# Experts in order of token count, and both parts of the activations in one stationary operand for three of them

## The chip, the cores and the metric

The kernel runs on one core of a Trainium2 chip. The metric is the device time of one execution in microseconds. TensorE (PE, with its weight loads PEld), VectorE (DVE), ScalarE (ACT), GpSimd (POOL) and SyncE (SP, which only issues transfers here) run at the same time and wait for each other by semaphores.

## What is computed

Two layers of an encoder on 256 tokens of 1,024 columns. Each layer has a mixer; layer 0 has a dense network behind it, layer 1 a mixture of eight experts, and the change is in that alone:

```python
def moe_swiglu(h, router_w, w1, w3, w2):
    t = h.reshape(B * L, D)
    logits = (t @ router_w).astype(jnp.float32)
    top_val, top_idx = lax.top_k(logits, TOP_K)
    top_w = jax.nn.softmax(top_val, axis=-1)
    ...
    for e in range(N_EXPERTS):
        out = out + combine[:, e:e + 1] * swiglu(t, w1[e], w3[e], w2[e])
```

`TOP_K` is 2 and `N_EXPERTS` 8. `swiglu` is `(silu(h @ w1) * (h @ w3)) @ w2`, with 3,584 hidden columns per expert. All is float32.

## The kernel before

**Split operands.** A float32 operand is split into a high part in a reduced type and the rest, the low part. A product is then three matmuls: high by high, high by low, low by high. Weights come in tiles of 128 x 1,024 (512 KB, `raw`), loaded on SyncE's queue (`wload`, line 286). ScalarE casts the high part (`wh`, line 319) and VectorE subtracts it for the low part (`wl`, line 320). There are four buffers for each part in the expert stage, so a tile's cast waits until TensorE is done with the tile four before. `take` (line 377) splits ahead until four tiles are ready.

**Loads.** The order of the loads is the plan written by `plan_experts`. For the raw tiles there are 16 permanent buffers and, by `lend` (line 1730), others for a time; four of these serve until tile 640 of the 672, so loads run 20 tiles ahead in most of the stage.

**Gather.** An expert has 128 slots. `one_hot` (line 1668) makes, from each token's slot, a matrix of 0 and 1 on VectorE. `gather` (line 1775) multiplies the tokens with it, two experts at a time, which gives each expert's tokens as stationary operands `gx`, high and low. It runs as a side task, a step every few products, during the last three blocks of the expert ahead. Behind the first gather, `weights` (line 1743) makes the softmax weights and `total` (line 1735) the counts; if one expert has more than 128 tokens, `over` is set and a second pass is run under an `If`, which comes last in the program.

**Blocks.** For each expert `e` and each `b` of 7 blocks of 512 hidden columns there are 4 tiles of w1 and 4 of w3 (lines 1891 to 1893, 48 matmuls of 512 columns). `gated` makes the activations `ma`: a SiLU on ScalarE, a product on VectorE (line 1902). `turned` (line 1847) transposes those of the block before with four matmuls, casts the high part on ScalarE and subtracts on VectorE (line 1854). `down` (line 1814) multiplies them with 4 tiles of w2 into `my` (lines 1820 to 1822, 24 matmuls). At an expert's end `weighted` splits and scales the result (VectorE line 1830) and `scatter` adds it to the tokens with 8 matmuls and 4 adds on VectorE (line 1845), spread over the next expert's second block.

**Order.** TensorE, VectorE and ScalarE run in the order in which the code is written (`by_hand`); SyncE's order is the scheduler's.

## Time and profile before

| | |
|---|---|
| median of 3 runs | 1926.29 us (1923.55 to 1928.28) |
| the profiled execution | 1928.92 us, of which its span 1927.1 us |
| PE / PEld busy | 1877.5 us (97%) / 1575.1 us (82%) |
| DVE / ACT / POOL busy | 1609.8 us (84%) / 1329.1 us (69%) / 29.7 us (2%) |
| matmuls of lines 1891 to 1893 | 3 x 896, starting at 925.4 us |
| matmuls of lines 1820 to 1822 | 3 x 448 |
| low parts on DVE, line 320 | 893, 1222 ns in the mean |
| high parts on ACT, line 319 | 893, 1053 ns in the mean |
| HBM read | 528.02 MB, mean of the span 275 GB/s |

The span runs from the first to the last instruction. A matmul's own time overlaps with that of the next: its duration (some 0.39 us for 512 columns) is no price, the step from one start to the next is. The share of DMA engines' time can go over 1, since packets overlap.

### The profile page before, as it was taken

The page shows a single profiled execution, that of the slowest core. Times are in us where ns is not written, and L with a number is a line of the kernel's source. Part 1 is how long each engine was busy: PE and PEld are TensorE (multiplying, and loading weights), DVE is VectorE, ACT ScalarE, POOL GpSimd, SP SyncE. Part 2 cuts the span into 40 slices and gives each one's busy share as a digit, 9 for nine tenths or more (in the row PEclk, how much of TensorE's full clock was granted, in tenths as well). Part 3 has the DMA queues.
Part 4 walks back from the last instruction along what each step waited for, and adds up shares of the span by engine and source line. Part 5 has one row for each costly group of instructions (what it writes and reads, how often), then busy time and mean ns, then how long its engine had stood idle before and what let it go on. Part 6 is the DMA issues. An engine that isn't in the chain of part 4 may idle for free.

```text
span 1927.1 us, 32350 instructions
## 1 busy us (share of the span) xinstructions
PE 1877.5 (97%) x12152; PEld 1575.1 (82%) x12152; DVE 1609.8 (84%) x2013; ACT 1329.1 (69%) x1874; POOL 29.7 (2%) x54
## 2 busy tenths in 40 slices
PE   7999999999989999999999999999999999999997
PEld 6987788799879877787788888888888888888885
DVE  6887887777766888767899989999889998899997
ACT  4785466643356874675777787777877778877775
POOL 1000000000000000000000000000000000000000
PEclk9999999999999999999999999999999999999998
DMA  9545765478874457568899999999999999999993
GB/s 326 162 132 159 237 184 183 149 252 271 278 231 132 142 159 227 184 200 321 277 335 351 339 350 344 365 375 356 354 339 368 368 354 369 338 352 378 357 324 108
DMA packets 258018, 531.29 MB, mean 276 GB/s; under 512 B 22126, under 2 KB 45116, under 8 KB 257852
## 3 DMA queue, kind: packets, MB, share of 16 engines
q1 hardware_dynamic: 257500, 528.99, 79.6%
q8 instruction: 97, 1.59, 0.3%
q14 instruction: 69, 0.57, 0.1%
q0 software_dynamic: 192, 0.07, 0.0%
q10 hardware_dynamic: 160, 0.07, 0.0%
HBM read 528.02 MB, written 1.05 MB: 275 GB/s over the span
## 4 chain that ended last, share of the span: by engine, by line
PE 75%; DMA 9%; DVE 7%; ACT 6%; issue 2%; SPq 0%; POOL 0%; ACTq 0%; DVEq 0%; POOLq 0%
PE mo L1891 11%; PE mo L1893 11%; PE mo L1892 11%; PE my L1820 5%; PE my L1821 5%; PE my L1822 5%; PE pn L398 3%; PE pn L401 3%; DMA raw<-in_ffn_w 3%; PE pn L399 3%; DVE wl L320 3%; DMA raw<-in_adaln_w 3%; PE pt L437 2%; PE pt L438 2%; PE pt L439 2%
## 5 line engine op out<-in xcount | busy, mean ns | idle before, releaser
L320 DVE TENSOR_TENSOR wl<-raw,wh 128x1024 fp32r<-128x1024 f32 (+1 forms) x893 | 1076.8, 1222 | 164.6 <-ACT wh L319 127.6
L319 ACT CAST wh<-raw 128x1024 fp32r<-128x1024 f32 (+1 forms) x893 | 931.8, 1053 | 375.5 <-PE mo L1893 97.9
L1891 PE MATMUL mo<-wh,gx 128*128 128x512 f32 x896 | 357.0, 398 | 0.0
L1892 PE MATMUL mo<-wl,gx 128*128 128x512 f32 x896 | 351.0, 392 | 0.0
L1893 PE MATMUL mo<-wh,gx 128*128 128x512 f32 x896 | 350.9, 392 | 0.0
L1893 PEld LDWEIGHTS mo<-wh,gx 128*128 128x128 f32 x896 | 168.2, 188 | 38.6 <-ACT gx L1792 1.2
L1891 PEld LDWEIGHTS mo<-wh,gx 128*128 128x128 f32 x896 | 168.4, 188 | 34.7 <-ACT gx L1792 0.6
L1892 PEld LDWEIGHTS mo<-wl,gx 128*128 128x128 f32 x896 | 168.5, 188 | 34.5 <-DVE wl L320 0.2
L1820 PE MATMUL my<-wh,aTm 128*128 128x512 f32 x448 | 176.0, 393 | 0.0
L1821 PE MATMUL my<-wl,aTm 128*128 128x512 f32 x448 | 175.3, 391 | 0.0
L1822 PE MATMUL my<-wh,aTm 128*128 128x512 f32 x448 | 175.2, 391 | 0.0
L438 PE MATMUL pt<-xH,wl 128*128 128x256 f32 x576 | 164.1, 285 | 3.7 <-DVE wl L320 3.6
L437 PE MATMUL pt<-xH,wh 128*128 128x256 f32 x576 | 166.4, 289 | 0.0
L439 PE MATMUL pt<-xL,wh 128*128 128x256 f32 x576 | 163.6, 284 | 0.0
L398 PE MATMUL pn<-wh,xH 128*128 128x512 f32 x352 | 149.1, 424 | 0.0
L399 PE MATMUL pn<-wl,xH 128*128 128x512 f32 x352 | 138.6, 394 | 0.0
L401 PE MATMUL pn<-wh,xL 128*128 128x512 f32 x352 | 138.6, 394 | 0.0
L450 DVE SCALAR_TENSOR_TENSOR acc<-raw,scol,acc 128x512 f32<-128x512 f32 x140 | 104.7, 748 | 26.7 <-DMA raw<-in_adaln_w 25.1
L438 PEld LDWEIGHTS pt<-xH,wl 128*128 128x128 f32 x576 | 111.1, 193 | 4.9 <-DVE wl L320 4.7
L437 PEld LDWEIGHTS pt<-xH,wh 128*128 128x128 f32 x576 | 111.1, 193 | 0.3
L439 PEld LDWEIGHTS pt<-xL,wh 128*128 128x128 f32 x576 | 111.1, 193 | 0.0
L1822 PEld LDWEIGHTS my<-wh,aTm 128*128 128x128 f32 x448 | 84.1, 188 | 18.9
(451 smaller groups left out, 2515.2 us busy)
## 6 DMA issues: line engine op xcount, KB each, us to landing
raw<-in_moe_w SPq DMA_DIRECT2D x672, 512.0 KB, 5.3
raw<-in_w_in SPq DMA_DIRECT2D x128, 512.0 KB, 3.8
raw<-in_adaln_w SPq DMA_DIRECT2D x80, 512.0 KB, 4.5
raw<-in_ffn_w SPq DMA_DIRECT2D x66, 512.0 KB, 4.7
raw<-in_w_branch SPq DMA_DIRECT2D x24, 512.0 KB, 3.9
rawe<-in_adaln_w SPq DMA_DIRECT2D x16, 512.0 KB, 7.3
raw<-in_w_out SPq DMA_DIRECT2D x16, 512.0 KB, 4.3
x<-in_x SPq DMA_DIRECT2D x2, 512.0 KB, 6.4
```

What stands on the lines that cost most here:

```text
L319: S.copy(H, r)
L320: low = lambda: tt(L, r, H, op=OP.subtract)
L398: mm(o, xH[:, tb, k, :], H, start=k == 0, stop=False)
L437: mm(d, H[:, cs], xH[:, :, k, :], start=k == 0 and c % 2 == 0, stop=False, skip_group_check=True)
L438: mm(d, L[:, cs], xH[:, :, k, :], start=False, stop=False, skip_group_check=True)
L439: mm(d, H[:, cs], xL[:, :, k, :], start=False, stop=k == KD - 1, skip_group_check=True)
L1820: mm(y[hf], aT[:, 0, k, :], H[:, c], start=b == 0 and k == 0, stop=False)
L1821: mm(y[hf], aT[:, 0, k, :], L[:, c], start=False, stop=False)
L1822: mm(y[hf], aT[:, 1, k, :], H[:, c], start=False, stop=b == nb - 1 and k == 3)
L1891: mm(q, gH[:, k, :], H, start=k == 0, stop=False)
L1892: mm(q, gH[:, k, :], L, start=False, stop=False)
L1893: mm(q, gL[:, k, :], H, start=False, stop=k == KD - 1)
```

## The change

The experts are taken in another order. Expert 0 stays first; the others follow by falling token count. The new `order`, in the place of `total`, ranks the counts on VectorE, makes a permutation, writes the expert numbers into `idx` and puts slots, masks and weights into the new order. `expert_rows` loads weights by an address from a register, which SyncE reads from `idx`; the seven reads and the one of `over` stand in SyncE's order ahead of the 38th tile's load (w3, expert 0, block 3), whose buffer is that of the 11th tile.

The last three places (5 to 7) use 64 slots. Their one-hot matrix holds the 64 slots twice, so `gx`, and all products up to the activations, have each token in row s and again in row s + 64. `turned` then takes the high part from the first 64 columns and the low part from the second, into one stationary operand of 128 columns, and `down` has two matmuls, by the weights' high and low part, in place of three. The scatter adds both halves of the rows. `over` is now set if the largest count is over 128 or that of place 5 is over 64. The first gather is for expert 0 alone, since the order isn't known then, and the second for place 1 alone; three pairs follow.

```diff
-    def plan_experts():
+    def expert_rows(w, e, sorted_, c0, n, k0, kn):
+        if not (sorted_ and e):
+            return kview(A[w][0, e], c0, n, k0, kn)
+        if e not in which:
+            which[e] = nc.values_load(idx[0:1, e:e + 1], engines=(E.SP,), min_val=0, max_val=NE - 1)
+        return A[w][0, bass.ds(which[e], 1), k0 * P:(k0 + kn) * P, c0:c0 + n].rearrange("o (k p) n -> p (o k) n", p=P)
+    def plan_experts(sorted_):
...
                 for w in ("moe_w1", "moe_w3"):
-                    add(w, lambda k0, kn, w=w, e=e, b=b: kview(A[w][0, e], b * 512, 512, k0, kn), KD, 512)
+                    add(w, lambda k0, kn, w=w, e=e, b=b: expert_rows(w, e, sorted_, b * 512, 512, k0, kn), KD, 512)
...
-        def one_hot(slots, pr):
+        def one_hot(slots, m, es, half):
...
+                for j, e in enumerate(es):
+                    at, o = C("iota"), hot[tb][:, j, :]
+                    if e in half:
+                        at = at[:, None, 0:64].to_broadcast([P, 2, 64])
+                        o = o.rearrange("p (i s) -> p i s", i=2)
+                    ts(o, at, slots[:, tb, e:e + 1], m[:, tb, e:e + 1], op0=OP.is_equal, op1=OP.mult)
             return hot
...
-            hots = [one_hot(slot, 0)]
+            hots = [one_hot(slot, m01, (0,), ())]
...
-        def total():
+        slotP, m01P, combP = [cvT[:, i:i + 2 * NE].rearrange("p (t e) -> p t e", t=2) for i in (0, 16, 32)]
+        first_slot = cvT[:, 48:48 + NE]
+        BIG = 5
+        def order():
...
             o = ps("total", [P, NE])
             mm(o, ones, m01[:, 0, :], start=True, stop=False)
             mm(o, ones, m01[:, 1, :], start=False, stop=True)
-            V.tensor_reduce(most, o, axis=AX.X, op=OP.max)
-            ts(over, most, float(P) + 0.5, None, op0=OP.is_gt)
+            n, pos, at = [tl("cnt", [P, NE], "ms") for _ in range(3)]
+            V.tensor_copy(n, o)
+            V.tensor_reduce(most[:, 0:1], n, axis=AX.X, op=OP.max)
+            ts(n[:, 0:1], n[:, 0:1], 1024.0, None, op0=OP.add)
+            sq = lambda t: (t[:, None, :].to_broadcast([P, NE, NE]), t[:, :, None].to_broadcast([P, NE, NE]))
+            nf, ne = sq(n)
+            gt, ge = [tl("gt", [P, NE, NE], "gq") for _ in range(2)]
+            tt(gt, nf, ne, op=OP.is_gt)
+            tt(ge, nf, ne, op=OP.is_ge)
+            V.copy_predicated(gt, C("tri8").bitcast(U32).rearrange("p (e f) -> p e f", e=NE), ge)
+            V.tensor_reduce(pos, gt, axis=AX.X, op=OP.add)
+            ts(first_slot, pos, BIG - 0.5, -64.0, op0=OP.is_gt, op1=OP.mult)
+            ts(first_slot, first_slot, 128.0, None, op0=OP.add)
+            perm, u = [tl("perm", [P, NE, NE], "gq") for _ in range(2)]
+            tt(perm, sq(pos)[0], sq(C("iota")[:, 0:NE])[1], op=OP.is_equal)
+            tt(u, perm, sq(C("iota")[:, 0:NE])[0], op=OP.mult)
+            V.tensor_reduce(at, u, axis=AX.X, op=OP.add)
+            V.tensor_copy(idx, at)
+            u = tl("permn", [P, NE], "ms")
+            tt(u, perm[:, BIG, :], n, op=OP.mult)
+            V.tensor_reduce(most[:, 1:2], u, axis=AX.X, op=OP.add)
+            ts(most[:, 1:2], most[:, 1:2], 64.0, most[:, 0:1], op0=OP.add, op1=OP.max)
+            ts(over, most[:, 1:2], float(P) + 0.5, None, op0=OP.is_gt)
+            u = tl("permu", [P, 2, NE, NE], "l1")
+            for d, s in ((slotP, slot), (m01P, m01), (combP, combk)):
+                tt(u, perm[:, None, :, :].to_broadcast([P, 2, NE, NE]),
+                   s[:, :, None, :].to_broadcast([P, 2, NE, NE]), op=OP.mult)
+                V.tensor_reduce(d, u, axis=AX.X, op=OP.add)
...
-            slots = slot
+            slots, m, comb, half = slotP, m01P, combP, range(BIG, NE)
             if blk:
-                plan_experts()
-                slots = tl("slb", [P, 2, NE], "gs")
-                ts(slots, slot, float(-P * blk), None, op0=OP.add)
+                plan_experts(False)
+                slots, m, comb, half = tl("slb", [P, 2, NE], "gs"), m01, combk, ()
+                tt(slots, slot, first_slot[:, None, :].to_broadcast([P, 2, NE]), op=OP.subtract)
             nb = DE // 512
-            def gather(pr, every):
-
-                hot = hots.pop(0) if hots else one_hot(slots, pr)
-                if pr:
+            groups = deque(((0,), (1,), (2, 3), (4, 5), (6, 7)))
+            def gather(es, every):
+                if es[0]:
                     yield 16
-                gs = [[tl("gx", [P, KD, P], "e4", F32R) for _ in range(2)] for _ in range(2)]
-                hT = [tl("hT", [P, 2, P], "l1", F32R) for _ in range(2)]
+                n = len(es)
+                gs = [[tl("gx", [P, KD, P], "e4", F32R) for _ in range(2)] for _ in es]
+                hT = [tl("hT", [P, 2, P], "l1", F32R) for _ in es]
...
                 for k in range(0, KD, 2):
                     for part, src in enumerate((hH, hL)):
-                        o = ps("gx", [P, 2, 2, P])
+                        o = ps("gx", [P, 2, n, P])
                         for i in range(2):
                             for tb in range(2):
                                 mm(o[:, i], src[:, tb, (k + i) * P:(k + i) * P + P], hot[tb],
                                    start=tb == 0, stop=tb == 1)
-                        S.copy(gs[0][part][:, k:k + 2, :], o[:, :, 0, :])
-                        S.copy(gs[1][part][:, k:k + 2, :], o[:, :, 1, :])
+                        for j in range(n):
+                            S.copy(gs[j][part][:, k:k + 2, :], o[:, :, j, :])
                         if part == 0:
...
-                if pr == 0 and slots is slot:
+                if es[0] == blk == 0:
                     weights()
-                    total()
+                    order()
                     yield 8
                 ws = ps("ws", [P, 2])
-                o = ps("hTp", [P, 2, 2, P])
-                for j in range(2):
-                    e = 2 * pr + j
+                o = ps("hTp", [P, n, 2, P])
-                        mm(ws[:, j:j + 1], hot[tb][:, j, :].bitcast(F32), combk[:, tb, e:e + 1],
+                        mm(ws[:, j:j + 1], hot[tb][:, j, :].bitcast(F32), comb[:, tb, e:e + 1],
...
                     for hf in range(2):
                         c = slice(hf * 512, hf * 512 + 512)
-                        mm(y[hf], aT[:, 0, k, :], H[:, c], start=b == 0 and k == 0, stop=False)
-                        mm(y[hf], aT[:, 0, k, :], L[:, c], start=False, stop=False)
-                        mm(y[hf], aT[:, 1, k, :], H[:, c], start=False, stop=b == nb - 1 and k == 3)
+                        first, last = b == 0 and k == 0, b == nb - 1 and k == 3
+                        if e in half:
+                            mm(y[hf], aT[:, k, :], H[:, c], start=first, stop=False)
+                            mm(y[hf], aT[:, k, :], L[:, c], start=False, stop=last)
+                        else:
+                            mm(y[hf], aT[:, 0, k, :], H[:, c], start=first, stop=False)
+                            mm(y[hf], aT[:, 0, k, :], L[:, c], start=False, stop=False)
+                            mm(y[hf], aT[:, 1, k, :], H[:, c], start=False, stop=last)
...
-            def turned(t):
+            def turned(e, t):
                 q = ps("maT", [P, 4, P])
                 for k in range(4):
                     nc.tensor.transpose(q[:, k, :], t[:, k * P:k * P + P], ident)
+                if e in half:
+                    aT = tl("aTm", [P, 4, P], "m4", F32R)
+                    S.copy(aT[:, :, 0:64], q[:, :, 0:64])
+                    tt(aT[:, :, 64:128], q[:, :, 64:128], aT[:, :, 0:64], op=OP.subtract)
+                    return aT
                 aT = tl("aTm", [P, 2, 4, P], "m4", F32R)
                 S.copy(aT[:, 0], q)
...
-            first = gather(0, 1)
+            first = gather(groups.popleft(), 1)
             for e in range(NE):
                 for b in range(nb):
-                    if e % 2 and b == 4 and e + 1 < NE:
-                        more = Side(gather(e // 2 + 1, 4), 1)
-                    if e and e % 2 == 0 and b == 0:
+                    if b == 4 and groups and groups[0][0] == e + 1:
+                        more = Side(gather(groups.popleft(), 4), 1)
+                    if e and b == 0:
                         more.drain("gather")
...
-    plan_experts()
+    plan_experts(True)
```

On VectorE, around the counts of the first gather (`oh`, `rest` and `combk` belong to the softmax weights, `wl` is the low part of the next weight tile), there stood:

```order
L1764 TENSOR_TENSOR combk<-oh_10315,rest_10320 128x16
L1740 TENSOR_REDUCE most<-total_10335 128x1
L1741 TENSOR_SCALAR over<-most 128x1
L320 TENSOR_TENSOR wl_10341<-raw_9946,wh_10340 128x1024
L1902 TENSOR_TENSOR ma_10350<-ma_10350,mo_10284 128x512
```

and now stands:

```order
L1811 TENSOR_TENSOR combk<-oh_10303,rest_10308 128x16
L1760 COPY cnt_10326<-total_10323 128x8
L1761 TENSOR_REDUCE most<-cnt_10326 128x1
L1762 TENSOR_SCALAR cnt_10326<-cnt_10326 128x1
L1766 TENSOR_TENSOR gt_10332<-cnt_10326 128x64
L1767 TENSOR_TENSOR gt_10333<-cnt_10326 128x64
L1768 COPY_PREDICATED gt_10332<-cc,gt_10333 128x64
L1769 TENSOR_REDUCE cnt_10327<-gt_10332 128x8
L1771 TENSOR_SCALAR cvT<-cnt_10327 128x8
L1772 TENSOR_SCALAR cvT<-cvT 128x8
L1775 TENSOR_TENSOR perm_10340<-cnt_10327,cc 128x64
L1776 TENSOR_TENSOR perm_10341<-perm_10340,cc 128x64
```

with 12 more such operations behind, of which six have 128 elements a partition or reduce these, and only then the low part of the same weight tile.

On TensorE, in a block of one of the last experts, between the last tile of w3 (`mo`) and the second tile of w2, there stood:

```order
L1893 MATMUL mo_17738<-wh_17741,gx_16618 128x512
L1820 MATMUL my_17315<-wh_17753,aTm_17735 128x512
L1821 MATMUL my_17315<-wl_17754,aTm_17735 128x512
L1822 MATMUL my_17315<-wh_17753,aTm_17735 128x512
L1820 MATMUL my_17316<-wh_17753,aTm_17735 128x512
L1821 MATMUL my_17316<-wl_17754,aTm_17735 128x512
L1822 MATMUL my_17316<-wh_17753,aTm_17735 128x512
L1820 MATMUL my_17315<-wh_17764,aTm_17735 128x512
```

and now stands:

```order
L1953 MATMUL mo_18707<-wh_18710,gx_16721 128x512
L1872 MATMUL my_18457<-wh_18722,aTm_18704 128x512
L1873 MATMUL my_18457<-wl_18723,aTm_18704 128x512
L1872 MATMUL my_18458<-wh_18722,aTm_18704 128x512
L1873 MATMUL my_18458<-wl_18723,aTm_18704 128x512
L1872 MATMUL my_18457<-wh_18734,aTm_18704 128x512
```

that is, two matmuls per tile and half of the output in place of three.

## Rows read from the trace of the kernel before

**Rows 1.** Stretch, length, busy (count): PE, PEld, DVE, ACT, POOL; clock, DMA share, GB/s.
```profile
1500.00:1550.00 50.00, 50.00 (x226) 41.01 (x225) 46.24 (x42) 39.65 (x42) 0.00 (x0) 1.00 1.01 374
```

**Rows 2.** Timeline of PE over one block: start, length, line, operation, tiles, shape, count.
```profile
1499.73 0.39 PE L1820 MATMUL my<-wh,aTm 128*128 128x512 f32 x1
...
1503.83 0.40 PE L1891 MATMUL mo<-wh,gx 128*128 128x512 f32 x1
...
1509.34 0.60 PE L1851 MATMUL maT<-cc,ma 128*128 128x128 f32 x4
...
1520.81 0.40 PE L1891 MATMUL mo<-wh,gx 128*128 128x512 f32 x1
```

**Rows 3.** Waits from 880 us on: total us, times, longest us.
```profile
ACT wh L319 <- PE mo L1893: 97.9, 290, 0.8
...
ACT wh L319 <- DMA raw<-in_moe_w: 1.3, 4, 0.3
```

**Rows 4.** Timeline of DVE in plain blocks: start, length, last the idle time before.
```profile
1504.90 0.68 DVE L1902 TENSOR_TENSOR ma<-ma,mo 128x512 f32<-128x512 f32 x1
1505.50 4.99 DVE L320 TENSOR_TENSOR wl<-raw,wh 128x1024 fp32r<-128x1024 f32 x4
1510.60 0.69 DVE L1854 TENSOR_TENSOR aTm<-maT,aTm 128x512 fp32r<-128x512 f32 x1
...
1557.71 3.49 DVE L320 TENSOR_TENSOR wl<-raw,wh 128x1024 fp32r<-128x1024 f32 x3
```

**Rows 5.** Groups by line on DVE: count, busy us, mean ns, idle before.
```profile
L1845 DVE TENSOR_TENSOR acc<-acc,sc 128x512 f32<-128x512 f32 x32 | 21.8, 681 | 0.1
...
L1830 DVE SCALAR_TENSOR_TENSOR ywL<-my,wsl,ywH 128x512 fp32r<-128x512 f32 x16 | 11.3, 744 | 3.2 <-ACT ywH L1829 3.2
```

**Rows 6.** Timeline of DVE in the router, ahead of the experts.
```profile
920.22 0.17 DVE L1645 COPY lgs<-lg 128x8 f32<-128x8 f32 x1 [0.56 <-PE lg L1641]
...
921.33 0.17 DVE L1653 TENSOR_SCALAR m<-rank 128x8 f32<-128x8 f32 x1
...
922.67 1.11 DVE L1673 TENSOR_SCALAR hot<-cc,slot,m 128x128 fp32r<-128x128 f32 x4
```

**Rows 7.** Timeline of DVE at the total of the counts.
```profile
942.51 0.16 DVE L1740 TENSOR_REDUCE most<-total 128x1 f32<-128x8 f32 x1
...
942.78 1.23 DVE L320 TENSOR_TENSOR wl<-raw,wh 128x1024 fp32r<-128x1024 f32 x1
```

**Rows 8.** Waits from 936 to 972 us.
```profile
PEld mo L1892 <- DVE wl L320: 0.2, 1, 0.2
```

**Rows 9.** Timeline of PE: full-precision matmuls of 128 columns, reduced ones of 256.
```profile
252.62 1.61 PE L1313 MATMUL do<-dv,aT 128*128 128x128 f32 x13
...
927.16 0.64 PE L1790 MATMUL gx<-hot,hH 128*128 128x256 f32 x4
```

**Rows 10.** Stretches around a fall of the clock, columns as in rows 1.
```profile
363.00:367.40 4.40, 1.85 (x14) 1.42 (x13) 2.95 (x8) 3.99 (x11) 0.55 (x1) 1.00 0.02 4
367.40:371.00 3.60, 3.60 (x19) 3.60 (x20) 2.44 (x5) 2.02 (x5) 0.92 (x1) 0.56 0.00 0
```

**Rows 11.** Stretches with a full DMA queue, and the fastest plain one.
```profile
880.00:890.00 10.00, 9.86 (x52) 8.06 (x51) 8.16 (x12) 3.32 (x6) 0.00 (x0) 1.00 1.05 402
...
1260.00:1280.00 20.00, 20.00 (x94) 16.42 (x93) 18.51 (x17) 15.50 (x16) 0.00 (x0) 1.00 1.02 379
```

**Rows 12.** DMA issues: tile, queue, count, KB each, us to landing.
```profile
raw<-in_moe_w SPq DMA_DIRECT2D x672, 512.0 KB, 5.3
```

**Rows 13.** Instructions of SyncE: shortest, median, longest ns.
```profile
L286 SPq DMA_DIRECT2D raw<-in_moe_w x672: 327/368/1355, 871.6 to 1886.1; - x168
...
L1940 SPq TENSOR_LOAD <-over x1: 480/480/480, 1886.4 to 1886.4; - x1
```

**Rows 14.** Timeline of DVE and of PE at the end.
```profile
1905.37 3.60 DVE L320 TENSOR_TENSOR wl<-raw,wh 128x1024 fp32r<-128x1024 f32 x3
...
1911.73 0.39 PE L1822 MATMUL my<-wh,aTm 128*128 128x512 f32 x1
```

More of the change, by code (lines that the diff above doesn't have):

```diff
@@ L1606, in moe_pool_a @@
             slots_of[tag].append((a, b))
-    def plan_experts():
+    which = {}
+    idx = cst.tile([P, NE], I32, name="idx")
+    def expert_rows(w, e, sorted_, c0, n, k0, kn):
[5 more added lines that the diff above has]
+    def plan_experts(sorted_):
         nb = DE // 512
@@ L1666, in nat_lo @@
             tt(hL[:, tb, c], hns[tb, q].rearrange("p a b -> p (a b)"), hH[:, tb, c], op=OP.subtract)
-        def one_hot(slots, pr):
-            hot = [tl("hot", [P, 2, P], "l1", F32R) for _ in range(2)]
+        def one_hot(slots, m, es, half):
+            hot = [tl("hot", [P, len(es), P], "l1", F32R) for _ in range(2)]
             for tb in range(2):
-                for j in range(2):
-                    e = 2 * pr + j
-                    ts(hot[tb][:, j, :], C("iota"), slots[:, tb, e:e + 1], m01[:, tb, e:e + 1],
-                       op0=OP.is_equal, op1=OP.mult)
+                for j, e in enumerate(es):
[4 more added lines that the diff above has]
+                    ts(o, at, slots[:, tb, e:e + 1], m[:, tb, e:e + 1], op0=OP.is_equal, op1=OP.mult)
             return hot
@@ L1730, in moe @@
             lend([10000] * 16 + [70] * 2 + [640] + [131] * 2 + [640] * 3 + [84] + [60] * 2)
-        most = cst.tile([P, 1], F32, name="most")
+        most = cst.tile([P, 2], F32, name="most")
         over = cst.tile([P, 1], I32, name="over")
-        def total():
+        slotP, m01P, combP = [cvT[:, i:i + 2 * NE].rearrange("p (t e) -> p t e", t=2) for i in (0, 16, 32)]
+        first_slot = cvT[:, 48:48 + NE]
+        BIG = 5
+        def order():
             o = ps("total", [P, NE])
@@ L1766, in experts @@
         def experts(blk):
[L1768 removed]
+            slots, m, comb, half = slotP, m01P, combP, range(BIG, NE)
             if blk:
[L1770 to L1772 removed]
+                plan_experts(False)
+                slots, m, comb, half = tl("slb", [P, 2, NE], "gs"), m01, combk, ()
+                tt(slots, slot, first_slot[:, None, :].to_broadcast([P, 2, NE]), op=OP.subtract)
             nb = DE // 512
[L1775 to L1778 removed]
+            groups = deque(((0,), (1,), (2, 3), (4, 5), (6, 7)))
+            def gather(es, every):
+                hot = hots.pop(0) if hots else one_hot(slots, m, es, half)
+                if es[0]:
                     yield 16
[L1780 to L1781 removed]
+                n = len(es)
+                gs = [[tl("gx", [P, KD, P], "e4", F32R) for _ in range(2)] for _ in es]
+                hT = [tl("hT", [P, 2, P], "l1", F32R) for _ in es]
                 wsl = tl("wsl", [P, 2], "ms")
[L1783 to L1784 removed]
+                for j, e in enumerate(es):
+                    of[e] = gs[j], hT[j], wsl[:, j:j + 1]
                 for k in range(0, KD, 2):
                     for part, src in enumerate((hH, hL)):
[L1787 removed]
+                        o = ps("gx", [P, 2, n, P])
                         for i in range(2):
@@ L1796, in gather @@
                     yield every
-                if pr == 0 and slots is slot:
+                if es[0] == blk == 0:
                     weights()
-                    total()
+                    order()
                     yield 8
                 ws = ps("ws", [P, 2])
-                o = ps("hTp", [P, 2, 2, P])
-                for j in range(2):
-                    e = 2 * pr + j
+                o = ps("hTp", [P, n, 2, P])
+                for j, e in enumerate(es):
                     for tb in range(2):
-                        mm(ws[:, j:j + 1], hot[tb][:, j, :].bitcast(F32), combk[:, tb, e:e + 1],
+                        mm(ws[:, j:j + 1], hot[tb][:, j, :].bitcast(F32), comb[:, tb, e:e + 1],
                            start=tb == 0, stop=tb == 1)
@@ L1809, in gather, with down @@
                         nc.tensor.transpose(o[:, j, tb, :], hot[tb][:, j, :].bitcast(F32), ident)
-                for j in range(2):
+                for j in range(n):
                     S.copy(hT[j], o[:, j])
-                S.copy(wsl, ws)
-            def down(y, b, aT, then=None):
+                S.copy(wsl[:, 0:n], ws[:, 0:n])
+            def down(e, b, aT, then=None):
+                y = ys[e]
                 for k, H, L in pieces("moe_w2", 4):
@@ L1860, in end @@
                     ys[e] = [ps("my", [P, 512], "pg") for _ in range(2)]
[L1861 removed]
+                down(e, b, aT, then)
                 if b == nb - 1:
@@ L1910, in experts @@
                     if prev is not None:
-                        end(prev[0], prev[1], aT, 2, (lambda: aTs.append(turned(t))) if final else None)
+                        end(prev[0], prev[1], aT, 2, (lambda: aTs.append(turned(e, t))) if final else None)
                     if not final:
```

7 lines of the change are left out of this document (2 added, 5 removed).

## The prediction

> **What bounds the kernel now.** I read the busy time by stretch first. In the 50 us from 1500, a plain part of the expert stage, TensorE is busy all the time, VectorE 46.24 us, ScalarE 39.65 us, the clock is granted in full, and the DMA engines move 374 GB/s at a share of 1.01 [rows 1]. Three resources are near their end at once, so the order of the waits decides. The waits say that ScalarE waits for TensorE to give a weight buffer back (97.9 us, 290 times), and hardly ever for a transfer (1.3 us, 4 times) [rows 3]: TensorE sets the pace and the others follow it. The timeline of TensorE gives its prices [rows 2]. One block (one expert, 512 of its hidden columns) lasts from 1503.83 to 1520.81, 16.98 us, and holds 72 matmuls of 512 columns, 4 transposes and no gap. Eighteen matmuls of the product with w2 take 1503.83 - 1499.73 = 4.10 us, 0.228 us each. So a matmul that goes is worth 0.228 us as long as nobody else is late.
>
> **What goes.** Three experts have 7 blocks each, and each block loses 8 of its 24 matmuls with w2: 3 x 7 x 8 = 168 matmuls, 168 x 0.228 = **-38.3 us**. A block of these experts becomes 16.98 - 8 x 0.228 = 15.16 us on TensorE.
>
> **What is late next in such a block.** Each of the others must do the same 12 tiles of weights in 15.16 us.
> ScalarE's share of a block is 39.65 / 50 x 16.98 = 13.5 us; it fits.
> VectorE: 12 low parts, one product of the gate, one low part of the activations. Back to back the low parts take 3.49 / 3 = 1.16 us each; where ScalarE's casts come in between, 4.99 / 4 = 1.25 us [rows 4]. The gate's product is 0.68. The low part of the activations is 0.69 at 512 columns and now has 256, so between 0.35 and 0.69; I take 0.43, nearer to the half. Back to back the sum is 12 x 1.16 + 0.68 + 0.43 = 15.0 us, just under 15.16; at 1.25 it is 16.1. I take 1.16, since a late engine is one that finds its input ready.
> VectorE has more in two blocks of every expert: the adds of the scatter, 4 x 0.68 = 2.7 us, in the second one, and the two weighted outputs, 2 x 0.74 = 1.5 us, in the first one [rows 5]. With the scatter, VectorE needs 15.0 + 2.7 = 17.7 us against 15.16 + 8 x 0.228 = 17.0 on TensorE; with the weighted outputs 16.5 against 15.2. The scatters of three experts and the weighted outputs of two fall into shortened blocks: 3 x 0.7 + 2 x 1.3 = 4.7 us at most, nothing if the four buffers of split weights bridge it. I take **+3.0**.
> The transfers: 12 tiles of 512 KB are 6.29 MB, in 15.16 us 415 GB/s. Where its queue was full the kernel moved 402 GB/s [rows 11], which makes 15.65 us a block, 0.49 too slow, 21 x 0.49 = 10.3 us over the three experts. But the loads run 20 buffers ahead (16 for good and four until tile 640), which is 20 x 16.98 / 12 = 28.3 us, of which 5.3 go from issue to landing [rows 12]. The lead of 23 us is larger than 10.3, so I cost the transfers at **0**.
> The end: VectorE's last three low parts start at 1905.37 and end at 1908.97 and the last matmul of the last product starts at 1911.73 [rows 14]. The 16 matmuls that go from the last two products would put it at 1908.1, before its weights are split. VectorE ends some 0.3 us earlier than now and leaves three matmuls, so it starts at about 1908.7 + 0.2 + 2 x 0.228 = 1909.3 and 1.2 us of the 168 matmuls' worth are lost: **+1.2** (0 to 2).
>
> **What is added: the order.** The new function puts 23 small operations on VectorE where 2 stood, ahead of the next low part. Six such operations of the ranking, of 8 to 64 elements, go from 920.22 to 921.50, 0.21 us each; four of 128 elements take 1.11 us, 0.28 each [rows 6]. Seventeen are of the first kind and six of the second: 17 x 0.21 + 6 x 0.28 = 5.3 us. The two that go took 942.78 - 942.51 = 0.27 [rows 7]. Net 5.0 us (4 to 6.5). Nothing hides it: behind the same place TensorE already waits 0.2 us for that low part today [rows 8], so its store of split weights is used up there. **+5.0.** In that wait TensorE stands still for 5 us. From 363 to 367.4 it was busy for 1.85 of 4.40 us, and over the next 3.6 us the granted clock was 0.56 in the mean, that is some 3.2 us at 1.2 GHz in place of 2.4 [rows 10]. Half the clock for 3.2 us costs 1.6 us. **+1.6** (0 if the clock holds, 3.2 if it stays low twice as long).
>
> **What is added: one more gather.** The first two experts are gathered alone, each with 32 matmuls of 128 columns in place of 32 of 256 for both. Four of 256 columns take 0.64 us, of which the last has 0.28, so one each 0.12; no such matmul of 128 columns with the reduced type is in the trace. Below, it could cost half of 0.12; above, as much as one of 512, 0.23. The nearest row is the full-precision one, where every record has 128 columns: 13 in 1.61, (1.61 - 0.28) / 12 = 0.11 [rows 9]. I take that: 64 x 0.11 - 32 x 0.12 = **+3.2** (0 to 64 x 0.23 - 3.8 = 10.9). The Trainium skill prices a stream of load-and-multiply pairs of 128 columns at 81 ns (TensorE: Matmul & The Clock Gate, Back-to-back issue gap); by that estimate the term would be 64 x 0.081 - 3.8 = +1.3. No row here shows that price; the nearest is the 0.11 above, of another type.
> In the first block each step has half of ScalarE's copies now. That can only gain, by tenths of a microsecond a step; I cost it at 0.
>
> **What moves at no cost.** SyncE reads seven expert numbers and the overflow flag right behind the order instead of the flag at the end. A read takes 0.48 us, and with the register work behind it perhaps 0.8: 8 x 0.8 = 6.4 us, in which the loads behind stand. The first of them would have waited for the low part behind the order anyway, and has a lead of over 20 tiles; cover gone, 6 us at most. Seven of eight experts' 588 loads take a register for their address; an issue takes 0.37 us now, in 1.26 us per tile there is room for three times that [rows 13]. The narrower cast of the activations on ScalarE lies beside the matmuls with w3, as now.
>
> **Sum.** -38.3 + 3.0 + 1.2 + 5.0 + 1.6 + 3.2 = -24.3 us. The profiled execution took 1928.92 us, its span being 1927.1, and would take 1904.6. The median of the three runs is 1926.29, 2.6 lower than the profiled one, and a change in the expert stage carries over as it is: **1902 us**.
>
> **Rivals.**
> A. *The short matmuls are dear.* If a matmul of 128 columns costs as much as one of 512, the extra gather is 10.9 in place of 3.2: 1902 + 7.7 = 1909. Against it stands only the row of another type.
> B. *VectorE becomes the bound.* At 1.25 us per low part a shortened block is 16.1, not 15.16: 21 x 0.95 = 20 us, 1922; with half of it, 1912. For it: 46.24 of 50 us busy [rows 1]. Against: many of the present steps of 1.25 hold a wait for ScalarE.
> C. *The DMA engines become the bound.* At 379 GB/s, the best 20 us of the plain part [rows 11], a block is 16.6 us; 21 x 1.44 = 30 us, less the lead of 23: 1902 + 7 = 1909. Had the stage no lead, only 21 x 0.38 = 8.0 us would come from the shortened blocks, and 1926.3 - 8.0 + 9.8 = 1928. The 402 GB/s with a full queue speak against it. The Trainium skill puts a core's share of HBM at about 358 GB/s and the vendor's figure at 368 (DMA: Bandwidth & Descriptors, Specifications); by 368 a block would need an estimated 17.1 us, as long as now, nothing would be gained and the time would be 1926.3 + 9.8 = 1936. The trace disagrees, with 374 over 50 us and 402 over 10.
> D. *SyncE becomes the bound, and the kernel slower.* If issuing a load with an address from a register takes longer than the 1.41 us in which tiles are used today, the seven experts go at its pace: at 1.6 us per load 588 x 0.19 = 112 us more, about 2040. It eats the gain from 1.26 us on and turns the sign at some 1.45. For it: the longest issue of these loads is 1.36 us; against it: their median is 0.37 [rows 13].
> E. *The change doesn't do what it says.* If the sixth expert in the order had over 64 tokens, everything would run twice. The reference's inputs give the experts 31, 45, 104, 80, 61, 72, 33 and 86 tokens; the first stays first, so the sixth has 61. Nothing runs twice.
>
> **How the numbers follow.** The forecast, with TensorE as the bound and the short matmuls at 0.11, 0.51; A 0.24; B 0.10; C with the lead 0.08; C without it 0.03; D 0.03; E 0.01. Predicted is the forecast's 1902; with its own terms at their ends (no stall of the clock, no loss on VectorE; or all of them) it lies between 1893 and 1908. The range takes in A, C with the lead and half of B: 1892 to 1915; what is left out is the rest of B, D, E and C without a lead, about 0.15. A measurement of this kernel tells 0.3% (5.8 us) from no change. Faster: forecast, A, B and C with the lead, 0.93. Within 0.3%: C without the lead, 0.03. Slower: D and E, 0.04.
>
> **What would show it.** The period of a plain block of the last three experts should be 15.2 us, with ScalarE still waiting for TensorE; 15.7 to 16.6 with the low parts back to back and TensorE waiting for them is B, the same with ScalarE waiting for transfers is C. The first five experts' plain blocks should stay at 16.98. At the order TensorE should stand for some 5 us and the clock fall once. The 128-column gather should step by 0.11 us, in A by over 0.2. SyncE should still wait for free buffers, not issue without a pause. The forecast is wrong above all if the shortened blocks do not come near 15.2.

## The result, and the profile after

The changed kernel takes 1901.0 us in the median (1900.1 to 1902.2), the kernel before 1926.97 in the same comparison: a ratio of 0.9863, with an interval from 0.9844 to 0.9882. The forecast was 1902. The profiled execution has a span of 1899.4 us (1927.1 before). Most of the forecast's steps held. Under the good agreement lie two errors in opposite directions: some 3 us in the terms of the sum, and 4 to 8 us from something that the forecast didn't have. That the number came out within 1 us is luck. The experiments take the two apart.

I divide the expert stage into blocks by the start of the first matmul with w1 (lines 1951 and, before, 1891), and read it from the timeline of TensorE. All in us; "stage" is from the first such matmul to the end of the span. Ahead of it, the profiled runs below differ by up to 11.5 us (918.7 to 930.2) where their instructions are the same, so the stage tells more than the median. Part of it goes with the clock: up to 918 us the granted clock is 0.98 in the mean in e2's profiled execution, the longest ahead of the stage, and 1.00 in e6's, the shortest.

| kernel | median | stage | first expert | its 2nd block | plain block | shortened | shortened, scatter |
|---|---|---|---|---|---|---|---|
| before | 1926.97 | 1001.6 | 118.7 | 18.23 | 16.96 | | |
| after | 1901.0 | 972.3 | 129.0 | 25.09 | 16.81 | 15.0 | 18.03 |
| e1 32 bytes at the left | 1922.27 | 993.9 | 117.8 | 18.17 | 16.81 | | |
| e2 no 32 bytes | 1905.45 | 980.3 | 130.9 | 25.27 | 16.96 | 15.15 | 18.05 |
| e3 three products | 1935.3 | 1005.0 | 129.0 | 24.98 | 16.81 | | |
| e4 spread order | 1892.13 | 965.2 | 121.6 | 16.83 | 16.81 | 15.0 | 18.04 |
| e5 seven short | 1857.64 | 928.1 | 129.3 | 25.34 | 16.80 | 15.0 | 18.03 |
| e6 spread, 32 bytes at the right | 1890.95 | 965.4 | 121.6 | 16.83 | 16.81 | 15.0 | 18.04 |
| e7 fill the stall | 1896.55 | 969.8 | 126.4 | 17.83 | 16.81 | 15.0 | 18.03 |
| e8 32 bytes at the right | 1919.9 | 994.2 | 117.9 | 18.18 | 16.81 | | |
| e9, e10, e11 | 1929.53, 1927.8, 1926.74 | 1004.3, 1002.2, 1000.1 | 119.1, 118.9, 118.5 | 18.2 to 18.3 | 17.02, 16.98, 16.92 | | |

The busy time by stretch, as [rows 1], of the changed kernel at the order, in a plain part with three products and in the shortened part:

```profile
943.50:949.00 5.50, 1.77 (x8) 1.13 (x6) 4.88 (x25) 4.56 (x5) 0.00 (x0) 1.00 0.44 168
949.00:956.00 7.00, 6.09 (x19) 5.00 (x20) 5.83 (x6) 1.38 (x3) 0.00 (x0) 0.51 0.54 175
1500.00:1550.00 50.00, 50.00 (x228) 41.38 (x227) 46.49 (x43) 39.84 (x42) 0.00 (x0) 1.00 1.02 375
1700.00:1750.00 50.00, 50.00 (x227) 41.24 (x226) 49.22 (x48) 42.95 (x47) 0.00 (x0) 1.00 1.03 390
```

In the shortened part TensorE is still busy all the time and at the full clock; VectorE has risen from 46.49 to 49.22 of 50 us, the transfers from 375 to 390 GB/s. One shortened block on TensorE, as [rows 2]:

```profile
1708.87 0.40 PE L1951 MATMUL mo<-wh,gx 128*128 128x512 f32 x1
...
1723.88 0.39 PE L1951 MATMUL mo<-wh,gx 128*128 128x512 f32 x1
```

15.01 us. VectorE in it, as [rows 4]:

```profile
1711.08 0.68 DVE L1962 TENSOR_TENSOR ma<-ma,mo 128x512 f32<-128x512 f32 x1
1711.68 4.62 DVE L320 TENSOR_TENSOR wl<-raw,wh 128x1024 fp32r<-128x1024 f32 x4
1716.22 0.42 DVE L1910 TENSOR_TENSOR aTm<-maT,aTm 128x256 fp32r<-128x256 f32 x1
1716.55 9.62 DVE L320 TENSOR_TENSOR wl<-raw,wh 128x1024 fp32r<-128x1024 f32 x8
```

The low parts follow each other without a gap, 4.62 / 4 = 1.16 and 9.62 / 8 = 1.20 us each, and the shorter low part of the activations takes 0.42 (the forecast had 1.16 and 0.43). The block from one gate product to the next (1711.08 to 1726.09) is 15.0 us on VectorE too.

The waits from 880 us on, as [rows 3]:

```profile
ACT wh L319 <- PE mo L1953: 80.4, 242, 0.8
...
PEld mo L1952 <- DVE wl L320: 11.2, 15, 5.1
...
ACT wh L319 <- DMA raw<-in_moe_w: 2.3, 6, 0.8
```

ScalarE still waits for TensorE, and for a transfer six times. Of TensorE's waits for a low part, 5.1 us are one wait. It stands behind the order; TensorE and then VectorE there, as [rows 6 to 8]:

```profile
944.89 0.39 PE L1951 MATMUL mo<-wh,gx 128*128 128x512 f32 x1
949.91 0.80 PE L1952 MATMUL mo<-wl,gx 128*128 128x512 f32 x1 [4.64 <-DVE wl L320]
950.50 0.63 PE L1953 MATMUL mo<-wh,gx 128*128 128x512 f32 x1
```

```profile
943.50 0.16 DVE L1760 COPY cnt<-total 128x8 f32<-128x8 f32 x1
943.69 0.16 DVE L1761 TENSOR_REDUCE most<-cnt 128x1 f32<-128x8 f32 x1
...
948.44 0.29 DVE L1788 TENSOR_REDUCE cvT<-permu 128x16 f32<-128x128 f32 x1
948.64 1.22 DVE L320 TENSOR_TENSOR wl<-raw,wh 128x1024 fp32r<-128x1024 f32 x1
```

The 23 operations last from 943.50 to 948.64, 5.14 us (5.3 forecast). TensorE stands idle for 4.64 us, and then its matmuls step by 0.43 in place of 0.23: the granted clock of the 7 us behind is 0.51, its 1.2 GHz level.

SyncE's reads of the order, and its issues of the experts' loads, as [rows 13]:

```profile
L1616 SPq TENSOR_LOAD <-idx x7: 262/267/474, 946.2 to 949.9; - x7
```

```profile
L286 SPq DMA_DIRECT2D raw<-in_moe_w x672: 327/373/1297, 872.9 to 1862.5; - x168
L286 SPq FUSED_REGOPS  x588: 42/46/61, 1017.2 to 1861.5; - x196
L286 SPq MOVE raw<-in_moe_w x588: 29/29/37, 1017.3 to 1861.6; - x196
```

The issue itself keeps its price with an address from a register (0.373 us, 0.368 before), and two small instructions of 0.046 and 0.029 stand ahead of it: together 0.45 us of the 1.25 that a tile has in a shortened block.

### The profile page after: what moved, and what is told of

It reads as the page before. It is cut to its first block, busy times and chain, and to the rows that moved or that the text cites. A ratio compares the mean times of both kernels' runs of the same rounds, so it can differ in the third digit from the quotient of the medians.

```text
span 1899.4 us, 33296 instructions
## 1 busy us (share of the span) xinstructions
PE 1841.5 (97%) x12016; PEld 1547.4 (81%) x12016; DVE 1597.5 (84%) x2034; ACT 1321.2 (70%) x1875; POOL 28.1 (1%) x54
## 4 chain that ended last, share of the span: by engine, by line
PE 75%; DMA 9%; DVE 7%; ACT 6%; issue 2%; POOL 0%; SPq 0%; DVEq 0%; ACTq 0%; POOLq 0%
PE mo L1952 11%; PE mo L1951 11%; PE mo L1953 11%; PE pn L398 4%; PE pn L401 4%; PE pn L399 4%; PE my L1875 3%; PE my L1876 3%; PE my L1877 3%; DMA raw<-in_adaln_w 3%; DMA raw<-in_ffn_w 3%; DVE wl L320 3%; ACT wh L319 2%; PE my L1873 2%; PE my L1872 2%
## 5 line engine op out<-in xcount | busy, mean ns | idle before, releaser
L1951 PEld LDWEIGHTS mo<-wh,gx 128*128 128x128 f32 x896 | 168.9, 188 | 32.8 <-ACT gx L1842 0.5
L1875 PE MATMUL my<-wh,aTm 128*128 128x512 f32 x280 | 109.1, 390 | 0.0
L1876 PE MATMUL my<-wl,aTm 128*128 128x512 f32 x280 | 109.0, 389 | 0.0
L1877 PE MATMUL my<-wh,aTm 128*128 128x512 f32 x280 | 108.9, 389 | 0.0
L398 PEld LDWEIGHTS pn<-wh,xH 128*128 128x128 f32 x352 | 66.9, 190 | 19.3 <-issue 7.6
```

The lines of the kernel that those rows point to most:

```text
L398: mm(o, xH[:, tb, k, :], H, start=k == 0, stop=False)
L1875: mm(y[hf], aT[:, 0, k, :], H[:, c], start=first, stop=False)
L1951: mm(q, gH[:, k, :], H, start=k == 0, stop=False)
```

## The experiments

Four questions: why plain blocks fell to 16.81 us where the forecast had them unchanged (e1, e2, e8 to e11), what the short products are worth by themselves (e3), what the order costs and whether it must (e4, e6, e7), and whether VectorE or the transfers come next (e5).

**e1: 32 bytes in the kernel before.** The row of indices is a new tile in the pool of constants, and the pools on its side move up by 32 bytes; the fourth of the four pairs of split buffers lies in a pool that fills the memory from the other end and stays.

```diff
+    pad = cst.tile([P, NE], I32, name="idx")
     def plan_experts():
```

> The kernel before with nothing added but 32 unused bytes per partition in the pool of constants, where the change puts its row of indices. That moves three of the four buffers for high and for low parts, and all that lies above them, by 32 bytes against the fourth. Theory PLACE (the plain block fell from 16.96 to 16.81 us since the buffers moved): the plain block here takes 16.81, the eight experts lose about 1.06 us each, and the kernel takes about 1918.5 us. Theory STREAM (it fell through the changed instructions or the addresses read from registers): the block stays at 16.96 and the time at 1926 to 1927.

The plain block took 16.81 us, the stage 993.9 in place of 1001.6; the median, 1922.27, was 0.9978 of before (0.9967 to 0.999), 4 us short of what was expected, with the stage as expected. PLACE holds: the change's 32 bytes alone bring 7.7 us in the stage.

**e2: the change without the 32 bytes.**

```diff
-    idx = cst.tile([P, NE], I32, name="idx")
+    idx = cvT[:, 56:56 + NE].bitcast(I32)
```

> The changed kernel with the row of indices kept in a spare part of a tile that is there already, so that no buffer moves against the kernel before. Theory PLACE: plain blocks with three products go back from 16.81 to 16.96 us, those with two from 15.0 to about 15.15, and the time rises from 1901 to about 1909. Theory STREAM: 16.81, 15.0 and 1901.

16.96 and 15.15 us, a stage of 980.3, and 1905.45 us: 0.9875 of before (0.9844 to 0.9907). So the change as it is described is worth 21.2 us in the median and 1001.6 - 980.3 = 21.3 in the stage. The profiled execution is the slowest of e2's four (1912.32 us, the fastest 1899.54), and in its first block the clock is low for a time. The busy time from the stage's start, in e2 and in the changed kernel:

```profile
930.00:935.00 5.00, 4.98 (x22) 4.00 (x22) 4.09 (x5) 2.75 (x5) 0.00 (x0) 0.71 0.56 184
927.00:932.00 5.00, 4.98 (x30) 3.95 (x29) 5.00 (x6) 3.18 (x6) 0.00 (x0) 1.00 0.52 184
```

In the 10 us ahead of these stretches TensorE was busy alike (9.46 and 9.42 us), so no run shows why the clock fell in the one only. It makes e2's first block 16.13 us where the change and e3 to e6 have 15.1, so some 1 us of e2's stage does not come from the change.

**e3: the sort without short products.**

```diff
-            slots, m, comb, half = slotP, m01P, combP, range(BIG, NE)
+            slots, m, comb, half = slotP, m01P, combP, ()
```

> The changed kernel with three products with w2 and 128 slots for every expert: experts still sorted, expert 0 still gathered alone, addresses still from registers, buffers where the change put them. What it costs over the change is what the shortened products are worth. My reading: the blocks of the last three experts go back to 16.81 (18.7 with the scatter), which is 30.6 us on the experts and 2 at the end, so about 1933 us. Rival (the sort and the lone gather cost nearer the forecast's 9.8 us over the kernel before and the gain of the placement belongs to the short blocks): 1937. Second rival (the short products themselves gave little, and the time came from elsewhere): under 1920.

1935.3 us; the stage is 1005.0 - 972.3 = 32.7 us longer than with short products, which is my reading's 30.6 and 2. With the median at 34 more the rival's 1937 is no further off than my 1933; the stage decides for my reading. Sort and gather without the short products make the kernel slower than before: 1.0045 (1.0031 to 1.0059). Against e1, which has the 32 bytes too, the stage is 1005.0 - 993.9 = 11.1 us longer: that is the price of the order and the gather, forecast at 9.8.

**e4: the order in small pieces.** The function yields after each operation, weights and order together, and is driven by the count of matmul triples as the gathers are.

```diff
-        def order():
+        EVERY = 3
+        def order(every):
...
             V.tensor_copy(n, o)
+            yield every
             V.tensor_reduce(most[:, 0:1], n, axis=AX.X, op=OP.max)
+            yield every
...
-                    weights()
-                    order()
-                    yield 8
+                    yield from order(EVERY)
```

> The changed kernel with the 35 small VectorE operations of the routing weights and of the order issued one by one, three matmul triples apart at first and two apart later, over the first expert, in place of all in one spot. Theory BACKLOG (the 25.09 us of the second block are a stall of TensorE behind VectorE plus the lower clock that follows it): the second block takes 16.8 to 17.3, no fall of the clock there, the first expert about 121 to 122 in place of 129.0, the time 1893 to 1895 us. Rival (VectorE is full in these blocks, and each small operation costs its 0.2 us wherever it stands): each of the blocks grows by about 1 us, only the clock's share of 2 to 3 us comes back, and the time is 1898 or more.

The second block fell from 25.09 to 16.83 us; the first expert from 129.0 to 121.6, the time to 1892.13 (0.982 of before, 0.9792 to 0.9848). Theory BACKLOG holds. The timeline of VectorE there:

```profile
940.27 1.23 DVE L320 TENSOR_TENSOR wl<-raw,wh 128x1024 fp32r<-128x1024 f32 x1 [0.25 <-DMA raw<-in_moe_w]
941.42 0.16 DVE L1762 TENSOR_REDUCE most<-cnt 128x1 f32<-128x8 f32 x1
941.49 1.21 DVE L320 TENSOR_TENSOR wl<-raw,wh 128x1024 fp32r<-128x1024 f32 x1
942.62 0.15 DVE L1764 TENSOR_SCALAR cnt<-cnt 128x1 f32<-128x1 f32 x1
942.69 2.35 DVE L320 TENSOR_TENSOR wl<-raw,wh 128x1024 fp32r<-128x1024 f32 x2
```

A small operation that nobody behind it needs costs VectorE 0.07 us from its start to the next one's (941.42 to 941.49); in the chain of the order, where most need the one before, they step by 5.14 / 23 = 0.22 in the mean. Spread out, the work is not only hidden, it is less.

**e5: seven experts with 64 slots.**

```diff
-            slots, m, comb, half = slotP, m01P, combP, range(BIG, NE)
+            slots, m, comb, half = slotP, m01P, combP, range(1, NE)
```

> The changed kernel with 64 slots and two products with w2 for places 1 to 7 of the order in place of the last three; of experts with more than 64 tokens the tokens beyond the 64th are left out, so part of the output is missing. 49 blocks in a row ask for 6.29 MB in 15.0 us each, so the lead of the loads must be used up if the transfers are too slow. By TensorE alone the four more experts give 4 x 7 x 8 x 0.227 = 50.8 us less about 1.4 us per expert where VectorE does the scatter: about 1856 us. Theory TRANSFERS (rival C of the prediction, at 379 GB/s): an expert needs 44.0 MB / 379 = 116.2 us against some 112.2 on TensorE, seven experts owe 28 us, less a lead of 23: 1861, with ScalarE waiting for transfers in the last experts. At the 368 GB/s that the Trainium skill names as the vendor's figure (DMA: Bandwidth & Descriptors, Specifications) it would be 7 x 7.5 - 23 = 29 us more, an estimated 1885. Theory VECTOR (rival B): the plain short block is over 15.0 once many stand in a row, at 15.7 it is 1880.

1857.64 us in a single run, near TensorE's 1856, and shortened blocks of 15.0 to the last. Two views of the experts from 1060 us to 1810, the busy time and the wait for transfers:

```profile
1060.00:1810.00 750.00, 744.50 (x3411) 610.26 (x3410) 724.62 (x713) 632.67 (x733) 0.00 (x0) 1.00 1.03 389
```

```profile
ACT wh L319 <- DMA raw<-in_moe_w: 2.2, 7, 0.3
```

389 GB/s over 750 us, with 2.2 us of waiting in all: TRANSFERS as priced, at 379 GB/s and with ScalarE waiting in the last experts, falls, and so does VECTOR. What TRANSFERS says of the lead is borne out, though. The weight tiles from 1200 us to 1760, those that ScalarE casts, those that SyncE loads, and the time from issue to landing (shortest, median, longest):

```profile
L319 ACT CAST wh<-raw x426: 1037/1055/1085, 1199.3 to 1758.9; 128x1024 fp32r<-128x1024 f32 x142
L286 SPq DMA_DIRECT2D raw<-in_moe_w x419: 332/373/870, 1200.1 to 1759.4; - x140
DMA to landing us min/median/max: 5.4/10.5/11.4
```

Seven tiles more are cast than loaded (one in the kernel before, over the same stretch), and a load takes 10.5 us to land where it took 5.3 [rows 12]. At 560 / 426 = 1.31 us a tile this is an estimated 7 x 1.31 + 5.2 = 14 us of a lead of 20 x 1.31 - 5.3 = 21. The transfers are slower than TensorE in such blocks, and the lead pays for it; it lasts for these seven experts, and no run shows a longer row of them. The Trainium skill's limit of 358 GB/s of HBM for one core and the vendor's 368 (DMA: Bandwidth & Descriptors, Specifications) do not bind here: this kernel, which runs on one core, is above both for 750 us.

**e6: the order spread, and the gap set from the other side.** As e4, with e2's place for the indices and 32 unused bytes behind the fourth pair.

```diff
             oh = sm("oh")
+            pools["right"][1].tile([P, NE], F32, name="pad", tag="pad", bufs=1)
```

> The order spread over the first expert as in the experiment before it, the row of indices in a spare part of an older tile, and 32 unused bytes at the end of the last pool, so that the fourth buffer pair and twelve load buffers move down by 32 bytes and all else stands as in the kernel before. Theory DISTANCE (what counts is where the fourth pair lies against the other three): blocks at 16.81 and 15.0 us, and since nothing moves in the stages ahead of the experts, their time stays at about 923 us in the median in place of some 927: 1888 to 1889 us. Rival (what counts is the address of the three first pairs themselves): 16.96 and 15.15, about 1897.

16.81 and 15.0 us a block, so DISTANCE holds against its rival. The time, 1890.95 us (0.9812 of before, 0.9793 to 0.9832), is 1.2 below e4's, which five and four runs don't tell apart; that the stages ahead gain anything is not shown. e4 and e6 are both 9 to 10 us faster than the change, of which 7 lie in the stage.

**e7: TensorE kept at work during the order.**

```diff
                     order()
+                    fill = ps("fill", [P, 512])
+                    gH, gL = gs[0]
+                    for i in range(20):
+                        mm(fill, gH[:, 0, :], gH[:, 0:4, :].rearrange("p a b -> p (a b)"), start=i == 0, stop=i == 19)
                     yield 8
```

> The changed kernel with 20 matmuls of 512 columns, whose result nobody uses, put into TensorE's queue right behind the order's own two, so that TensorE works (some 4.6 us) while VectorE does the order. Theory CLOCK (of the 8.3 us by which the second block is longer than a plain one, some 4.7 are the stall and the rest the lower clock behind it): the granted clock stays at 1.00 there, the stall's length stays, and the second block falls from 25.09 to about 22.5; the time to about 1898.5. Rival (the matmuls behind the stall are slow for another reason, cold buffers or a late VectorE): the block stays near 25, or grows by what the 20 matmuls take, and the time is 1901 or more.

The matmuls ran ahead of the second block, so it is the sum of the first two that counts: 19.68 + 17.83 = 37.51 us against 15.09 + 25.09 = 40.18. The same two stretches as above:

```profile
943.50:949.00 5.50, 5.39 (x28) 4.23 (x27) 5.33 (x11) 3.48 (x6) 0.00 (x0) 1.00 0.02 4
949.00:956.00 7.00, 7.00 (x34) 5.79 (x33) 6.99 (x8) 5.68 (x9) 0.00 (x0) 1.00 0.97 339
```

The clock stays at 1.00 and 2.7 us come back, though TensorE does 4.5 us of useless work. CLOCK holds: the fall behind the stall costs 2.7 us. (1896.55 us, from 1890 to 1903.5 in four runs.)

**e8 to e11: which distance?** The kernel before, with the pool of the fourth pair moved, in which twelve of the load buffers lie too: e8 has the unused tile alone (32 bytes down), e9 one small buffer less (64 up), e10 both (32 up), e11 two buffers less and the tile (96 up).

```diff
-        NB["gs"] = 11
+        NB["gs"] = 10
...
             oh = sm("oh")
+            pools["right"][1].tile([P, NE], F32, name="pad", tag="pad", bufs=1)
```

> The kernel before with 32 unused bytes at the end of the last pool alone: the fourth buffer pair and twelve load buffers move down by 32 bytes, all else stays. DISTANCE: plain blocks of 16.81 in place of 16.96, the stages ahead of the experts as they were, 1918.5 us. Rival (the address of the three first pairs counts): 16.96 and 1926 to 1927.

> The kernel before with the fourth buffer pair and twelve load buffers 64 bytes higher (one small buffer of 64 bytes less ahead of the top of the memory), all else in place. Before, the fourth pair lies 121632 bytes above the first, 32 more than a multiple of 64; here 121696, still 32 more. Theory MULTIPLE OF 64 (the two good placements so far, 121600, are one, and the bad one is not): the block stays at 16.96 and the time at 1926 to 1927. Rival ANY OTHER PLACE (the present distance is a bad one by accident, and nearly any other is better): 16.81 and 1918 to 1920.

> The kernel before with the fourth pair and twelve load buffers 32 bytes higher, all else in place: distance 121664, a multiple of 64 and not of 128. MULTIPLE OF 64: the block takes 16.81 and the kernel 1918 to 1920. If a multiple of 128 is needed (121600 is one): 16.96 and 1926.

> The kernel before with the fourth buffer pair and twelve load buffers 96 bytes higher (two small buffers less and 32 unused bytes more), all else in place: the distance to the first pair is 121728 bytes, 951 times 128. Theory MULTIPLE OF 128 (121600 took 16.81 us a block at two different places, 121632, 121664 and 121696 took 16.96 to 17.02): 16.81 and 1918 to 1920 us. Rival (the distance of 121600 alone is a good one, or the two good kernels share something else): 16.96 or more and 1926 to 1930.

e8 took 16.81 us a block and 1919.9 us (0.9962, 0.9947 to 0.9976); e9 17.02 and 1929.53, e10 16.98 and 1927.8, e11 16.92 and 1926.74, all three the same as before or a little longer. So ANY OTHER PLACE falls, since 121632, 121664, 121696 and 121728 bytes are all worse than 121600; MULTIPLE OF 64 falls with e10 and MULTIPLE OF 128 with e11. What the rule is stays open; a distance of 121600 was good at two places of the whole. Nor does a run tell the fourth pair from the twelve load buffers, which move with it. How the time is lost is plain from a block start in e8 and in e9:

```profile
1323.46 0.39 PE L1892 MATMUL mo<-wh,gx 128*128 128x512 f32 x1
...
1324.59 0.39 PE L1894 MATMUL mo<-wh,gx 128*128 128x512 f32 x1
...
1340.27 0.39 PE L1892 MATMUL mo<-wh,gx 128*128 128x512 f32 x1
```

```profile
1322.13 0.40 PE L1891 MATMUL mo<-wh,gx 128*128 128x512 f32 x1
...
1323.31 0.40 PE L1893 MATMUL mo<-wh,gx 128*128 128x512 f32 x1
...
1339.15 0.40 PE L1891 MATMUL mo<-wh,gx 128*128 128x512 f32 x1
```

Five steps take 1.13 us in e8, 0.226 each, and 1.18 in e9, 0.236 each, with the same instructions, the same engines at work beside them and no wait. In the kernel before, the first 11 or so matmuls of a tile group step like this, with w1 and with w2, and the rest by 0.227. In e8 these two groups step by 0.227 throughout, but the first ten or so matmuls with w3, behind the four transposes, still step by 0.224 to 0.236: the distance takes away some of the slow steps, not all.

## Why the prediction was right

Placement aside, the terms compare like this, by the stage, in two pairs of kernels: without the 32 bytes (e2 against before) and with them (after against e1).

| term | forecast | e2 against before | after against e1 | from |
|---|---|---|---|---|
| 168 matmuls less, VectorE late, the end | -38.3 + 3.0 + 1.2 = -34.1 | -33.5 | -32.8 | start of the sixth expert to that of the last block 351.3 to 319.7 and 348.5 to 317.8, from there on 38.1 to 36.1 and 38.0 to 35.9 |
| the order's stall and the clock | +5.0 + 1.6 = +6.6 | +7.0 | +6.9 | second block 18.23 to 25.27 and 18.17 to 25.09 |
| the lone gather | +3.2 | +5.2, some 1.0 of it e2's clock | +4.3 | first block +0.5 and -0.5, fifth to seventh +4.7 and +4.8 |
| sum | -24.3 | -21.3 | -21.6 | |
| the 32 bytes | none | | -8 in the stage, some 1 of it e2's clock | e2 to after, 980.3 to 972.3 |

**What goes**, and what is late next. Right by its steps: shortened blocks of 15.15 us without the 32 bytes (15.16 worked out in the text), VectorE back to back at 1.16 to 1.20 and not at 1.25. With the scatter the block takes 18.03, and the one behind it some 0.2 more than a plain one; TensorE's own work is 15.0 + 8 x 0.227 = 16.8. The scatters in the seventh and eighth expert thus cost 2 x 1.45 = 2.9 us, the forecast's 3.0; the one in the sixth, the first with shortened blocks, costs next to nothing in its own block (16.88). The weighted outputs, half of the bound of 4.7, cost nothing: the block with them takes 15.05. The end:

```profile
1879.51 3.49 DVE L320 TENSOR_TENSOR wl<-raw,wh 128x1024 fp32r<-128x1024 f32 x3
```

```profile
1883.62 0.40 PE L1873 MATMUL my<-wl,aTm 128*128 128x512 f32 x1
```

The last low part ends at 1883.0 and the last matmul starts 0.6 later; the forecast had 0.66, where 2.8 us lay between them [rows 14].

**The order.** The stall was 4.64 us for a forecast of 5.0. The clock's part was sized 1.6 and is 2.7 (e7): the stretch [rows 10] from which it was taken had 3.2 us at the lower level, here it is nearly all of 7. The step was right and its size off; the bound of 3.2 held.

**The gather** is the term that was missed, by 1 us (after against e1; e2's first block, with its low clock, makes it look like 2). Its matmuls cost about what the forecast said:

```profile
928.73 0.56 PE L1839 MATMUL gx<-hot,hH 128*128 128x128 f32 x4
929.13 0.61 PE L1839 MATMUL gx<-hot,hL 128*128 128x128 f32 x4
929.76 0.50 PE L1951 MATMUL mo<-wh,gx 128*128 128x512 f32 x1
...
1044.73 0.50 PE L1854 MATMUL ws<-cvT,hot 128*128 128x1 f32 x4
1045.59 0.44 PE L1857 MATMUL hTp<-cc,hot 128*128 128x128 f32 x2 [0.36 <-DVE aTm L1914]
1045.79 0.48 PE L1951 MATMUL mo<-wh,gx 128*128 128x512 f32 x1
```

Four of 128 columns from 928.73 to 929.13, 0.10 us each (0.11 forecast), and the four behind them, up to the next long matmul, 0.16; rival A, at 0.23, falls. But the gather of expert 1 alone has a tail of its own, the weights' products and the transposes, from 1044.73 to 1045.79, 1.06 us with a wait inside, which the sum left out; some 0.5 more lies in long matmuls that follow short ones and step by more than 0.227. The Trainium skill's 81 ns for a load-and-multiply pair of 128 columns in a stream (TensorE: Matmul & The Clock Gate, Back-to-back issue gap), given there without the type, is not reached here: the least is the 0.10 above.

**At no cost.** SyncE's reads started from 946.2 to 949.9 and left no trace in the waits for transfers; its issues stayed at 0.373 us (rival D falls). Transfers at 0 was right, and for the reason given, the lead. In the last experts of the changed kernel, from 1700 us to 1800, a load takes 10.3 us to land, where it took 5.3 [rows 12]:

```profile
raw<-in_moe_w SPq DMA_DIRECT2D x78, 512.0 KB, 10.3
```

So the transfers fall behind there, at 390 GB/s for a forecast of 402, and nobody waits for them, since the loads run ahead. In e5 the lead bridges even seven such experts. By the time rival C falls in all three forms, and B with it; that the transfers are slower than the shortened blocks, on which C rests, is so. E did not happen.

**Plain blocks of 16.98 in the first five experts** was wrong: 16.81. The prediction read the block's period as matmuls times a duration and did not ask why many stepped by 0.23 and others by 0.227. Had it known, it would have said 1894 and been 7 low in the median, since of the 8 us in the stage only some 4 show in the medians of e1 and of e2 against after; where the rest is, ahead of the experts or in the spread of runs, is not settled. In e8, where only the pool of the fourth pair moves, the median fell by the whole 7.9, which points to the stages ahead.

## What to carry over

Where TensorE, VectorE and the transfers are all within some 7% of their ends, a cut on the one that sets the pace can still be forecast, when the others' prices are taken from back-to-back rows and not from means that hold waits, and when a lead that covers a slower engine is held against the length of the stretch: it is used up, not free. Small operations that prepare a later step belong between the large ones of many blocks and not in one place: in one place they cost their chain, a stall and the clock behind it (7 us of the stage here), between the others almost nothing. After a change that adds a tile, compare the step of untouched matmuls before crediting the change: 32 bytes moved 8 us.

## What was not expected of the hardware

A 512-column matmul steps by 0.227 us or by up to 0.24, with nothing waiting, depending on where the pool of the fourth buffer pair and of twelve load buffers lies to the other three pairs in SBUF. That the accesses of several engines meet in SBUF there is my guess; no run shows the mechanism. The Trainium skill says that on the engines' side of SBUF only the port pair shared by VectorE and GpSimd causes contention, and that TensorE and ScalarE never wait on anyone (SBUF — State Buffer, SBUF: two separate sides). GpSimd is idle in these blocks, so by that rule my guess is wrong and the cause another; that the place of a buffer matters, e1, e2, e8 and e9 show.
